# Spreading the second block's top 16, cutting the convolution into pieces, and a norm column that holds epsilon

## The chip, the cores and the metric

One core of a Trainium2 chip runs the whole kernel in one launch. The metric is the device time of that launch in microseconds (us). Five engines work side by side, each through its own queue in order: TensorE (PE in the profile; its weight loads are PEld), VectorE (DVE), ScalarE (ACT), GpSimd (POOL) and SyncE (SP), which issues most of the DMA transfers.

## The reference

Two blocks of two layers each work on x, 256 tokens of 1024 channels, in float32. What matters for the change:

```python
def _layer(x, ...):                      # the first block, layers l0 and l1
    h = _rms_norm(x, norm_g)             # x * rsqrt(mean(x*x) + 1e-6) * g
    proj = h @ w_in                      # a, a_glu, z_conv, c_q, ..., u_sg, v_sg, z_sg
    y_conv = _conv_branch(a, a_glu, ...) * silu(z_conv)   # 31 taps, causal, depthwise
    y_mla = _mla_branch(...) * silu(z_mla)
    y_sg = _sgu_branch(u_sg, v_sg, ...) * silu(z_sg)
    y = concat([rms_norm(y_conv), rms_norm(y_mla), rms_norm(y_sg)])
    return x + y @ w_out

def peer_ffn(h, w_q, sub_keys, u_tab, v_tab):   # the second block, twice
    scores = einsum(h @ w_q, sub_keys)
    s1, i1 = top_k(scores[..., 0, :], 16);  s2, i2 = top_k(scores[..., 1, :], 16)
    top_s, top_pos = top_k(s1[:, None] + s2[None, :], 16)   # per token and head, of 8 heads
    gate = softmax(top_s)                # 16384 experts, 128 chosen per token
    act = gelu(einsum(u_tab[idx], h))
    return einsum(gate * act, v_tab[idx])
```

The second block runs: norm, hgrn2 mixer, norm, peer; norm, rglru ("lru") mixer, norm, peer; and a last norm. The modulation vectors of its layers (`cond @ w_ada + b_ada`) do not depend on x.

## The kernel before, in words

The stages are l0, l1, hg, p0, lru, p1 and fin. x lies in one tile for the whole run, in two blocks b of 128 tokens. Weights come through a ring of four 1 MB slots (`wp`, tile w) and a ring of twelve 4 KB-per-partition buffers (`rp`, tile r). Outside the peer loops the order of each engine's queue is planned when the program is built: of the instructions that are ready, the one that stands first in the program goes first; `behind()` queues a group behind the last instructions that `mod_hT` or `split_T` marked.

**A norm of x** (`rms_x`, lines 301 to 307): ScalarE squares the block and sums it (line 305), GpSimd scales the sum and adds epsilon (line 166, in `pow`), then raises it to -0.5 (line 170); VectorE multiplies x by it (line 313). There are 14: two blocks in each of l0, l1, hg, p0, lru, p1 and fin; the two of fin end in line 1471.

**A layer of the first block** (`first_layer`, 457 to 576). A weight unit `W(u)` is split into a high and a low half (ScalarE line 226, VectorE line 227), for three matmuls per product (254 to 256). Behind the attention's inputs come the spatial gate's projections (`sgu`), the scores, then `conv` (729 to 743): 31 taps for two halves of the channels, 62 VectorE instructions in a chain (737, 740). Behind it in the program stand three gate units (9, 10, 11: two weight splits each), `values` with the softmax's transposes, unit 6, the branch norms and products (`branch`, 553 to 565), modulation rows (`ada`, line 267), and `conv_out` (745 to 777), which needs the convolution's result cv from line 755 on. `out_proj` ends the layer.

**The peer stage** (`peer`, 1174 to 1461) ends in two loops of 128 units written out in order under `manual_schedule`. In the u loop, unit j loads 128 rows of the u table (half of a 1 MB slot), TensorE multiplies it with the last 160 tokens (line 1335), ScalarE applies gelu (`u_act`). The first 96 tokens (`TS`) instead fetch their own 128 rows each through GpSimd's indirect DMA (`fetch`, line 1293, six ahead) and take them one row of 128 at a time on VectorE (`own`, line 1305), paced by unit. Each fetch takes a buffer of `rp`. Block 1's top 16 also runs within this loop: for each head, `keys` (VectorE's maxima and indices, then sums of candidates on GpSimd, lines 1104 to 1117) and `sums` (1123 to 1127); then `slot_rows` (1142 to 1159, two buffers of `rp`), `slot_weights` (exponential on ScalarE, line 1133; VectorE 1134 to 1136), and `slot_columns(1)` on TensorE (1166, 1170). `own_rows(r)` copies a group of tokens on ScalarE into a buffer of `rp` (1276, 1277) and turns it on TensorE (1281). From unit `G0` on, `hot`, `meet` and `put` set the expert weights of four tokens every second unit. The v loop follows (line 1434).

The lru stage's steps (line 1079) each begin with one modulation unit, two instructions of line 267, from the third step on.

Of the kernel before, what the change touches and what calls it, by code (L numbers as in the profile page):

```python
# [137 lines left out]
class Kernel:  # L138
# [35 lines left out]

    def setup(self):
        nc, A, k = self.nc, self.A, self.keep
        self.x = self.t(k, (P, 2, D), "x")
        self.mhalf = self.t(k, (P, 1), "mhalf")
        nc.vector.memset(self.mhalf, -0.5)

        nc.scalar.activation(self.t(k, (P, 1), "warm"), self.mhalf, AF.Square)
        for b in range(2):
            nc.sync.dma_start(self.x[:, b], A["x"][b * P:(b + 1) * P])
        self.cst = self.t(k, (P, NCONST - 1024), "cst")
        nc.scalar.dma_start(self.cst[:, :256], A["consts"][:, :256])
        self.cols = self.t(k, (P, NCOLS), "cols")
        nc.scalar.dma_start(self.cols, A["cols"])
        self.ident = self.cst[:, K_ID:K_ID + P]
        self.mask = self.cst[:, K_MASK:K_MASK + P]
        self.iota = self.cst[:, 256:256 + P]  # L190
        self.cos = self.cst[:, K_COS - 1024:K_COS - 1024 + 32].rearrange("p (b h) -> p b h", b=2)
        self.sin = self.cst[:, K_SIN - 1024:K_SIN - 1024 + 32].rearrange("p (b h) -> p b h", b=2)
        self.c31 = self.t(k, (P, 8), "c31", U32)
        nc.vector.memset(self.c31, 31)
        self.ones = self.t(k, (P, S), "ones")
        nc.vector.memset(self.ones, 1.0)
        self.mod = [self.t(k, (P, 48), f"mod{l}") for l in range(2)]
        self.ada_todo = [(l, j) for l in range(2) for j in range(0, 48, 2)]
        self.cond = None
# [98 lines left out]
        at = R1[(name, layer)] - R1[("conv_pw_b", layer)]  # L298
        return self.rows[:, at:at + n]

    def rms_x(self, b, out):

        nc = self.nc
        rs = self.t(self.keep, (P, 1), "rs", bufs=2)
        nc.scalar.activation(out, self.x[:, b], AF.Square, accum_out=rs)  # L305
        self.rstd(rs, rs, D)
        return rs

    def norm_x(self, b):

        xn = self.rp.tile([P, D], F32, name="r")
        rs = self.rms_x(b, xn)
        self.nc.vector.tensor_scalar(xn, self.x[:, b], rs, None, op0=ALU.mult)
        return xn

    def mod_hT(self, pool, l, h, hT=None, parts=True):
# [140 lines left out]
    def first_layer(self, l):  # L457
        nc, tc = self.nc, self.tc
        W = lambda u: self.w3(f"win{l}", u * SLOT)
        with tc.tile_pool(name=f"l{l}", bufs=1) as pl, tc.tile_pool(name=f"m{l}", bufs=2) as pm:  # L460
# [75 lines left out]
            with tc.tile_pool(name=f"b{l}", bufs=1) as pb:  # L536
                y = self.t(pb, (P, 2, D), "y")
                zc = self.t(pb, (P, 2, 256), "zc")
                z = self.t(pb, (P, 2, 768), "z")
                sgu = self.sgu(l, pb, pm, wm, wuv)  # L540
                sc, rl = self.scores(pb, pm, qT, kT, rq)
                cv = self.conv(l, pb, yp)
                def gate_unit(u, dst):

                    w = W(u)
                    for b in range(2):
                        nc.scalar.activation(dst[:, b], self.proj3(w, b), AF.Copy)

                for n in range(3):
                    gate_unit(9 + n, z[:, :, n * 256:(n + 1) * 256])  # L550
                yT = self.t(pb, (P, 8, S), "yT")

                def branch(c0, n):

                    for b in range(2):
                        ys = y[:, b, c0:c0 + n]
                        zs = z[:, b, c0 - 256:c0 - 256 + n] if c0 else zc[:, b]
                        nc.scalar.activation(zs, zs, AF.Silu)
                        nc.vector.tensor_tensor(ys, ys, zs, op=ALU.mult)
                        junk = self.t(pl, (P, D), "junk", BF16)  # L560
                        ss = self.t(pm, (P, 1), "bss")
                        nc.scalar.activation(junk[:, :n], ys, AF.Square, accum_out=ss)
                        self.rstd(ss, ss, n)
                        nc.vector.tensor_scalar(ys, ys, ss, None, op0=ALU.mult)
                        self.transpose_T(ys, yT, c0 // P, n // P, b, lambda c: self.col("branch_norm_g", c, l))

                self.values(pm, sc, rl, v, y)
                gate_unit(6, zc)
                branch(256, 512)
                sgu(y)  # L570
                self.ada(ADA[l][1])
                branch(768, 256)
                self.conv_out(l, pb, cv, wm, y)
                branch(0, 256)
                self.ada(len(self.ada_todo) - (34, 18)[l])
                self.out_proj(f"wout{l}", yT, (1, 2, 3, 0), 1)
# [150 lines left out]
                                            rl[:, hs, b:b + 1].to_broadcast([P, 2, 64]), op=ALU.mult)  # L727

    def conv(self, l, pl, yp):
        nc = self.nc  # L730
        cv = self.t(pl, (P, 2, S), "cv")
        o = [None, None]
        for j in range(31):
            for f in range(2):
                dst = cv[:, f] if j == 30 else self.t(pl, (P, S), f"cvb{f}", bufs=2)
                if j == 0:
# [3 lines left out]
                    nc.vector.scalar_tensor_tensor(dst, yp[:, f, j:j + S], self.col("conv_w", f * 31 + j, l), o[f],  # L740
                                                   op0=ALU.mult, op1=ALU.add)
                o[f] = dst
        return cv

    def conv_out(self, l, pl, cv, wm, y):

# [246 lines left out]
    def lru(self):  # L993
        nc, tc = self.nc, self.tc
        first = [self.w1("lruin", n * SLOT) for n in range(2)]
        with tc.tile_pool(name="lr", bufs=1) as pl, tc.tile_pool(name="lrm", bufs=2) as pm:
# [81 lines left out]
            heads = self.proj_blocks(first, mT)  # L1078
            for step in "x0 x1 x2 g0 x3 y0 y1 g1 d0 s0 y2 y3 d1 s1".split():
                k, n = step[0], int(step[1])  # L1080
                self.ada(1 if step not in ("x0", "x1") else 0)
                if k == "x":
                    x_unit(n)
                elif k == "y":
                    y_unit(n)
                elif k == "g":
                    gates(n, 0)
                    gates(n, 1)
                elif k == "d":
                    decay(n)  # L1090
                else:
                    for f in range(4):
                        scan(n, f)
# [80 lines left out]
    def peer(self, l):  # L1174
# [9 lines left out]
        with ExitStack() as ctx:  # L1184
# [132 lines left out]
            with tc.manual_schedule():  # L1317
# [56 lines left out]

                NG = TD // 4
                AHEAD = 6
                G0 = 34
                k = 0
                for j in range(P):
                    u_mm(j)  # L1380
                    if j in (2, 26):
                        b = j // 26
                        late = self.slot_rows(pn, tif[b], ts[b], tp[b])
                    if j:
                        u_act(j - 1)
                    if j in (6, 30):
                        self.slot_weights(pn, late[0])

                    for f, at in ((sums, (9, 12, 14, 16, 19, 21, 23, 25)), (keys, (7, 9, 12, 14, 17, 19, 21, 23))):
                        if j in at:  # L1390
                            f(at.index(j), 1)
                    if j == 9:
# [5 lines left out]
                            fetch(i)  # L1398
                    if j == 12:
                        own_rows(0)  # L1400
                    if j == 32:
                        self.slot_columns(1, *late, slots)
                        c1.close()
                        wts["b"] = self.t(pool("pw"), (P, P - JW, TD), "Wb")
                    if j in (40, 72):
                        own_rows(1 if j == 40 else 2)
                    if j >= 13 and k < TS and (j - 13) * TS >= k * 112:
                        own(k)
                        fetch(k + AHEAD)
# [53 lines left out]
    def final(self, out):  # L1463
# [3 lines left out]
        nc.scalar.dma_start(rows, bass.AP(tensor=r.tensor, offset=r.offset + R_FINAL, ap=[[0, P], [1, D]]))  # L1467
        for b in range(2):
            o = self.rp.tile([P, D], F32, name="r")
            rs = self.rms_x(b, o)  # L1470
            nc.vector.scalar_tensor_tensor(o, self.x[:, b], rs, rows, op0=ALU.mult, op1=ALU.mult)  # L1471
            nc.sync.dma_start(out[b * P:(b + 1) * P], o)

# [37 lines left out]
```

## Time and profile before

| | us |
|---|---|
| median of three runs | 2140.9 (2137.68 to 2143.72) |
| the profiled execution | 2138.78 |
| its span | 2137.1 |
| mean granted TensorE clock in it | 0.969 of full speed |

The profile is one execution. A view of waits names, for each engine, which instruction of another engine released it; a timeline lists instructions by start, merged where equal ones follow each other, with the idle time before them and what ended it in brackets; the table of stretches gives each engine's busy time between two times. L12 is line 12 of the kernel.

### The profile page before, as it was taken

How to read it: one execution, taken by the hardware profiler on the slowest of the kernel's cores; microseconds unless marked ns; L12 is line 12 of the kernel's file. 1: busy time of each engine (PE TensorE's matmuls, PEld its weight loads, DVE VectorE, ACT ScalarE, POOL GpSimd, SP SyncE). 2: the span in 40 equal slices, each digit the busy share in tenths (PEclk: the TensorE clock that was granted, in tenths of full speed). 3: DMA queues.
4: the chain of work that ended last, by engine and by line, in shares of the span. 5: the costliest groups of instructions: out<-in, count | busy, mean ns of one | idle time of the engine just before them, and what ended most of it. 6: DMA issues, size and time to landing. Idle time of an engine off the chain costs nothing. (4 is left out here: it accounts for less than half of the span.)

```text
span 2137.1 us, 35449 instructions
## 1 busy us (share of the span) xinstructions
PE 1997.6 (93%) x13860; PEld 1871.6 (88%) x13860; DVE 1402.8 (66%) x3072; ACT 630.4 (29%) x1697; POOL 636.1 (30%) x696
## 2 busy tenths in 40 slices
PE   6978978999999979999999997999979999999997
PEld 6664777788869979999999997969979999999997
DVE  7697687587648776788444446967786788544444
ACT  4442462354523224432000001754224433000000
POOL 0202111011001464444344440001373444244442
PEclk9989999999999989999999998999989999999999
DMA  9537617443413899999999999643799999999996
GB/s 347 219 149 283 240 64 308 148 140 95 149 50 139 339 339 367 343 369 389 368 414 415 415 415 387 247 154 119 263 357 371 354 360 378 370 416 415 415 415 267
DMA packets 123719, 630.01 MB, mean 295 GB/s; under 512 B 13728, under 2 KB 14368, under 8 KB 79264
## 3 DMA queue, kind: packets, MB, share of 16 engines
q1 hardware_dynamic: 66960, 422.87, 51.4%
q0 software_dynamic: 55296, 201.35, 24.4%
q10 hardware_dynamic: 1296, 3.53, 0.5%
q8 instruction: 109, 1.79, 0.3%
q14 instruction: 58, 0.48, 0.1%
HBM read 626.65 MB, written 1.05 MB: 294 GB/s over the span
## 5 line engine op out<-in xcount | busy, mean ns | idle before, releaser
L1335 PE MATMUL ps<-hT,w 128*128 128x160 f32 x4096 | 573.0, 299 | 0.3 <-issue 0.2
L1335 PEld LDWEIGHTS ps<-hT,w 128*128 128x128 f32 x4096 | 560.3, 190 | 0.8 <-issue 0.8
L1314 DVE SCALAR_TENSOR_TENSOR hl<-r,asl,hl 128x1024 f32<-128x1024 f32 x186 | 239.1, 1285 | 312.5 <-DMA r<-v,ids 302.9
L1434 PE MATMUL acc<-Wa,w 128*128 128x160 f32 x2560 | 348.4, 299 | 0.0
L1434 PEld LDWEIGHTS acc<-Wa,w 128*128 128x128 f32 x2560 | 347.9, 190 | 0.0
L1293 POOL DMA_INDIRECT r<-v,ids x192 | 240.2, 1251 | 339.7 <-PE acc L1434 263.6
L1293 POOL DMA_INDIRECT r<-urow,ids x192 | 257.7, 1342 | 260.4 <-DVE r L1305 138.0
L1305 DVE SCALAR_TENSOR_TENSOR r<-r,hh 128x1024 f32<-128x1024 f32 x192 | 232.5, 1219 | 1.4 <-DMA r<-urow,ids 1.4
L1434 PE MATMUL acc<-Wb,w 128*128 128x160 f32 x1536 | 209.6, 299 | 0.3 <-DMA w<-v 0.3
L1434 PEld LDWEIGHTS acc<-Wb,w 128*128 128x128 f32 x1536 | 208.8, 190 | 0.5 <-DMA w<-v 0.5
L1453 ACT ACTIVATE hT<-acc,mod 128x256 f32<-128x256 f32 x8 | 3.5, 474 | 573.5 <-DVE hT L1455 573.5
L1355 ACT ACTIVATE r<-r,hl 128x128 f32<-128x128 f32 x320 | 102.2, 390 | 224.2 <-DVE r L1352 224.2
L254 PE MATMUL ps<-hh,r 128*128 128x256 f32 (+1 forms) x464 | 135.4, 292 | 5.3 <-ACT r L226 4.2
L256 PE MATMUL ps<-hh,r 128*128 128x256 f32 (+1 forms) x464 | 132.8, 286 | 6.0 <-DVE r L227 6.0
L255 PE MATMUL ps<-hl,r 128*128 128x256 f32 (+1 forms) x464 | 132.9, 287 | 0.5 <-DVE hl L377 0.5
L227 DVE TENSOR_TENSOR r<-w,r 128x1024 fp32r<-128x1024 f32 (+1 forms) x82 | 96.9, 1201 | 32.3 <-ACT r L226 30.5
L267 DVE SCALAR_TENSOR_TENSOR w<-w,crow 128x1024 f32<-128x1024 f32 x96 | 114.0, 1219 | 2.9 <-ACT crow L819 2.1
L226 ACT ACTIVATE r<-w 128x1024 fp32r<-128x1024 f32 (+1 forms) x82 | 83.6, 1037 | 80.0 <-PE ps L255 33.9
L1352 DVE TENSOR_TENSOR r<-cst,hl 128x1024 f32<-128x1024 f32 x80 | 97.6, 1220 | 0.0
L254 PEld LDWEIGHTS ps<-hh,r 128*128 128x128 f32 (+1 forms) x464 | 88.8, 192 | 7.1 <-ACT r L226 5.0
L256 PEld LDWEIGHTS ps<-hh,r 128*128 128x128 f32 (+1 forms) x464 | 88.4, 191 | 7.2 <-DVE r L227 6.9
L255 PEld LDWEIGHTS ps<-hl,r 128*128 128x128 f32 (+1 forms) x464 | 88.7, 192 | 1.4 <-DVE hl L377 0.8
(382 smaller groups left out, 2930.2 us busy)
## 6 DMA issues: line engine op xcount, KB each, us to landing
w<-u SPq DMA_DIRECT2D x128, 1024.0 KB
w<-v SPq DMA_DIRECT2D x128, 1024.0 KB
w<-ada SPq DMA_DIRECT2D x48, 1024.0 KB
w<-win SPq DMA_DIRECT2D x24, 1024.0 KB
r<-hgin SPq DMA_DIRECT2D x40, 512.0 KB
w<-wq SPq DMA_DIRECT2D x12, 1024.0 KB
r<-wout SPq DMA_DIRECT2D x16, 512.0 KB
r<-wmid SPq DMA_DIRECT2D x12, 384.0 KB
```

The costliest lines, as they stand in the source:

```text
L227: self.nc.vector.tensor_tensor(lo, x, hi.bitcast(F32), op=ALU.subtract)
L254: mm(ps, a[0], b[0], start=start, stop=False)
L255: mm(ps, a[0], b[1], start=False, stop=False)
L256: mm(ps, a[1], b[0], start=False, stop=stop)
L267: nc.vector.scalar_tensor_tensor(x, x, 1.0, self.cond, op0=ALU.mult, op1=ALU.mult, accum_out=m[:, j + i:j + i + 1])
L1293: g = nc.gpsimd.indirect_dma_start(out=x, out_offset=None, in_=A[f"urow{l}"] if k < TS else vrow, in_offset=at)
L1305: nc.vector.scalar_tensor_tensor(x, x, 1.0, hrep[r % 2], op0=ALU.mult, op1=ALU.mult, accum_out=asl[:, g:g + 1])
L1314: nc.vector.scalar_tensor_tensor(accs[r % 2], x, asl[:, g:g + 1], accs[r % 2], op0=ALU.mult, op1=ALU.add)
L1335: nc.tensor.matmul(ps, u[:, c], hT[:, c, TS:], start=c == 0, stop=c == 7)
L1352: nc.vector.tensor_tensor(o, self.iota[:, None, None].to_broadcast([P, 2, 4, P]), slots[:, 1:3, k:k + 4, None].to_broadcast([P, 2, 4, P]), ...
L1355: nc.scalar.activation(o[:, 1, t], o[:, 1, t], AF.Copy, scale=slots[:, 0, k + t:k + t + 1])
L1434: mm = nc.tensor.matmul(acc[c // 2][:, c % 2, TS:], v[:, c * P:(c + 1) * P], W(j), start=j == 0 and c % 2 == 0, stop=False, skip_group_che ...
```

## The change

x gets eight more columns; the first of them holds the root of 1024 times epsilon, so that the Square's sum over 1025 columns already has epsilon in it, and the constant factor goes into the multiplication that follows (or, in fin, into a small instruction of VectorE). `conv` returns a function that issues a given number of its 31 steps; `first_layer` calls it behind each of three gate units (6 each), behind unit 6 (7) and behind the first branch (6). In the lru stage the modulation units are queued behind `mod_hT`'s last instructions. In the u loop block 1's `sums` and `keys` are spread to unit 28 in place of 25, `slot_rows` moves from unit 26 to 29, `slot_weights` from 30 to 34, `slot_columns` from 32 to 39, `own_rows(1)` from 40 to 37, and `G0` from 34 to 40.

```diff
--- before.py
+++ after.py
@@ -174,11 +174,14 @@
 
     def setup(self):
         nc, A, k = self.nc, self.A, self.keep
-        self.x = self.t(k, (P, 2, D), "x")
+
+        self.xe = self.t(k, (P, 2, D + 8), "x")
+        self.x = self.xe[:, :, :D]
         self.mhalf = self.t(k, (P, 1), "mhalf")
         nc.vector.memset(self.mhalf, -0.5)
 
         nc.scalar.activation(self.t(k, (P, 1), "warm"), self.mhalf, AF.Square)
+        nc.gpsimd.memset(self.xe[:, :, D:D + 1], (D * EPS) ** 0.5)
         for b in range(2):
             nc.sync.dma_start(self.x[:, b], A["x"][b * P:(b + 1) * P])
         self.cst = self.t(k, (P, NCONST - 1024), "cst")
@@ -298,19 +301,20 @@
         at = R1[(name, layer)] - R1[("conv_pw_b", layer)]
         return self.rows[:, at:at + n]
 
-    def rms_x(self, b, out):
+    def rms_x(self, b):
 
         nc = self.nc
         rs = self.t(self.keep, (P, 1), "rs", bufs=2)
-        nc.scalar.activation(out, self.x[:, b], AF.Square, accum_out=rs)
-        self.rstd(rs, rs, D)
+        sq = self.rp.tile([P, SLOT], BF16, name="r")[:, :D + 1]
+        nc.scalar.activation(sq, self.xe[:, b, :D + 1], AF.Square, accum_out=rs)
+        nc.gpsimd.tensor_tensor(rs, rs, self.mhalf, op=ALU.pow)
         return rs
 
     def norm_x(self, b):
 
         xn = self.rp.tile([P, D], F32, name="r")
-        rs = self.rms_x(b, xn)
-        self.nc.vector.tensor_scalar(xn, self.x[:, b], rs, None, op0=ALU.mult)
+        rs = self.rms_x(b)
+        self.nc.vector.tensor_scalar(xn, self.x[:, b], rs, float(D) ** 0.5, op0=ALU.mult, op1=ALU.mult)
         return xn
 
     def mod_hT(self, pool, l, h, hT=None, parts=True):
@@ -539,7 +543,8 @@
                 z = self.t(pb, (P, 2, 768), "z")
                 sgu = self.sgu(l, pb, pm, wm, wuv)
                 sc, rl = self.scores(pb, pm, qT, kT, rq)
-                cv = self.conv(l, pb, yp)
+                cv, conv = self.conv(l, pb, yp)
+
                 def gate_unit(u, dst):
 
                     w = W(u)
@@ -548,6 +553,7 @@
 
                 for n in range(3):
                     gate_unit(9 + n, z[:, :, n * 256:(n + 1) * 256])
+                    conv(6)
                 yT = self.t(pb, (P, 8, S), "yT")
 
                 def branch(c0, n):
@@ -566,7 +572,9 @@
 
                 self.values(pm, sc, rl, v, y)
                 gate_unit(6, zc)
+                conv(7)
                 branch(256, 512)
+                conv(6)
                 sgu(y)
                 self.ada(ADA[l][1])
                 branch(768, 256)
@@ -727,10 +735,17 @@
                                             rl[:, hs, b:b + 1].to_broadcast([P, 2, 64]), op=ALU.mult)
 
     def conv(self, l, pl, yp):
+
         nc = self.nc
         cv = self.t(pl, (P, 2, S), "cv")
-        o = [None, None]
-        for j in range(31):
+        o, left = [None, None], list(range(31))
+
+        def steps(n):
+            for j in left[:n]:
+                step(j)
+            del left[:n]
+
+        def step(j):
             for f in range(2):
                 dst = cv[:, f] if j == 30 else self.t(pl, (P, S), f"cvb{f}", bufs=2)
                 if j == 0:
@@ -740,7 +755,8 @@
                     nc.vector.scalar_tensor_tensor(dst, yp[:, f, j:j + S], self.col("conv_w", f * 31 + j, l), o[f],
                                                    op0=ALU.mult, op1=ALU.add)
                 o[f] = dst
-        return cv
+
+        return cv, steps
 
     def conv_out(self, l, pl, cv, wm, y):
 
@@ -1078,7 +1094,9 @@
             heads = self.proj_blocks(first, mT)
             for step in "x0 x1 x2 g0 x3 y0 y1 g1 d0 s0 y2 y3 d1 s1".split():
                 k, n = step[0], int(step[1])
-                self.ada(1 if step not in ("x0", "x1") else 0)
+                if step not in ("x0", "x1"):
+                    with self.behind():
+                        self.ada(1)
                 if k == "x":
                     x_unit(n)
                 elif k == "y":
@@ -1374,19 +1392,19 @@
 
                 NG = TD // 4
                 AHEAD = 6
-                G0 = 34
+                G0 = 40
                 k = 0
                 for j in range(P):
                     u_mm(j)
-                    if j in (2, 26):
-                        b = j // 26
+                    if j in (2, 29):
+                        b = j // 29
                         late = self.slot_rows(pn, tif[b], ts[b], tp[b])
                     if j:
                         u_act(j - 1)
-                    if j in (6, 30):
+                    if j in (6, 34):
                         self.slot_weights(pn, late[0])
 
-                    for f, at in ((sums, (9, 12, 14, 16, 19, 21, 23, 25)), (keys, (7, 9, 12, 14, 17, 19, 21, 23))):
+                    for f, at in ((sums, (10, 13, 15, 18, 20, 23, 25, 28)), (keys, (7, 10, 13, 15, 18, 20, 23, 25))):
                         if j in at:
                             f(at.index(j), 1)
                     if j == 9:
@@ -1398,12 +1416,12 @@
                             fetch(i)
                     if j == 12:
                         own_rows(0)
-                    if j == 32:
+                    if j == 39:
                         self.slot_columns(1, *late, slots)
                         c1.close()
                         wts["b"] = self.t(pool("pw"), (P, P - JW, TD), "Wb")
-                    if j in (40, 72):
-                        own_rows(1 if j == 40 else 2)
+                    if j in (37, 72):
+                        own_rows(1 if j == 37 else 2)
                     if j >= 13 and k < TS and (j - 13) * TS >= k * 112:
                         own(k)
                         fetch(k + AHEAD)
@@ -1467,7 +1485,8 @@
         nc.scalar.dma_start(rows, bass.AP(tensor=r.tensor, offset=r.offset + R_FINAL, ap=[[0, P], [1, D]]))
         for b in range(2):
             o = self.rp.tile([P, D], F32, name="r")
-            rs = self.rms_x(b, o)
+            rs = self.rms_x(b)
+            nc.vector.tensor_scalar(rs, rs, float(D) ** 0.5, None, op0=ALU.mult)
             nc.vector.scalar_tensor_tensor(o, self.x[:, b], rs, rows, op0=ALU.mult, op1=ALU.mult)
             nc.sync.dma_start(out[b * P:(b + 1) * P], o)
 

```

## Rows read from the trace of the kernel before

**Rows 1.** What TensorE waited for: for whom, us in all, times, longest.

```profile
PE ps L255 <- DVE r L227: 30.2, 2, 15.1
PE ps L1166 <- DVE wk L1136: 29.0, 2, 15.3
```

**Rows 2.** Timeline of VectorE, layer 0: start us, us, engine, line, operation, count.

```profile
129.17 6.73 DVE L740 SCALAR_TENSOR_TENSOR cvb<-yp,cols,cvb 128x256 f32<-128x256 f32 x17
...
136.61 6.90 DVE L227 TENSOR_TENSOR r<-w,r 128x1024 fp32r<-128x1024 f32 x6
...
176.41 0.75 DVE L755 SCALAR_TENSOR_TENSOR cv<-ps,cv 128x256 f32<-128x256 f32 x2
```

**Rows 3.** Stretches: us, busy per engine, granted clock, DMA share, GB/s.

```profile
core 0: us, PE busy (x) PEld busy (x) DVE busy (x) ACT busy (x) POOL busy (x), PEclk, DMA share, GB/s
122.84:203.00 80.16, 61.37 (x328) 44.62 (x329) 66.19 (x150) 28.29 (x68) 10.17 (x15) 0.87 0.65 252
137.89:142.00 4.11, 4.11 (x19) 4.11 (x20) 4.11 (x4) 0.00 (x0) 0.00 (x0) 0.51 0.47 146
309.40:385.80 76.40, 58.59 (x324) 43.59 (x324) 59.32 (x140) 26.60 (x67) 8.26 (x14) 0.89 0.68 257
771.20:776.80 5.60, 5.59 (x40) 5.54 (x41) 5.60 (x11) 0.68 (x2) 4.68 (x4) 0.50 0.88 290
1100.00:1150.00 50.00, 50.00 (x373) 50.00 (x372) 21.31 (x17) 0.00 (x0) 23.11 (x18) 1.00 1.02 414
1339.00:1400.00 61.00, 61.00 (x362) 56.04 (x361) 60.88 (x111) 44.64 (x63) 0.39 (x4) 1.00 0.65 243
```

**Rows 4.** Timeline of TensorE, first peer stage, around its gap.

```profile
739.71 16.19 PE L1335 MATMUL ps<-hT,w 128*128 128x160 f32 x118
771.21 0.45 PE L1166 MATMUL ps<-cst,wk 128*128 128x128 f32 x1 [15.31 <-DVE wk L1136]
```

**Rows 5.** Timeline of VectorE, first peer stage, before that gap ends.

```profile
756.90 0.24 DVE L1123 MAX8 ts<-cand 128x8 f32<-128x80 f32 x1 [0.78 <-POOL cand L1115]
...
769.08 1.22 DVE L1305 SCALAR_TENSOR_TENSOR r<-r,hh 128x1024 f32<-128x1024 f32 x1
...
770.23 0.28 DVE L1134 TENSOR_REDUCE wsm<-wk 128x8 f32<-128x128 f32 x1
```

**Rows 6.** Timeline of GpSimd, same stage: one fetch.

```profile
768.28 1.68 POOL L1293 DMA_INDIRECT r<-urow,ids  x1 [1.28 <-DVE r L1305]
```

**Rows 7.** Timeline of ScalarE, same stage: the copies of `own_rows(1)`.

```profile
793.32 0.84 ACT L1276 ACTIVATE r<-hT 128x768 f32<-128x768 f32 x1
794.05 0.41 ACT L1277 ACTIVATE r<-hT 128x256 f32<-128x256 f32 x1
```

**Rows 8.** The norms: timelines, groups by line, one line's durations (ns min/median/max).

```profile
2127.95 0.19 POOL L166 TENSOR_SCALAR rs<-rs 128x1 f32<-128x1 f32 x1 [26.99 <-ACT r L305]
2128.23 0.57 POOL L170 TENSOR_TENSOR rs<-rs,mhalf 128x1 f32<-128x1 f32 x1
2128.99 1.18 POOL L166 TENSOR_SCALAR rs<-rs 128x1 f32<-128x1 f32 x1 [0.19 <-ACT r L305]
...
2128.84 1.28 DVE L1471 SCALAR_TENSOR_TENSOR r<-x,rs,w 128x1024 f32<-128x1024 f32 x1 [1.56 <-POOL rs L170]
...
L166 POOL TENSOR_SCALAR rs<-rs 128x1 f32<-128x1 f32 x14 | 6.3, 451 | 180.3 <-ACT r L305 180.2
...
L313 DVE TENSOR_SCALAR r<-x,rs 128x1024 f32<-128x1024 f32 x12 | 9.0, 753 | 14.0 <-POOL rs L170 14.0
...
L894 DVE TENSOR_SCALAR hbE<-hf x4: 685/1112/1541, 415.5 to 520.1; 128x1024 f32<-128x1024 f32 x4
```

**Rows 9.** Timeline of VectorE, lru stage: first and last of ten, then line 227.

```profile
1309.81 1.22 DVE L267 SCALAR_TENSOR_TENSOR w<-w,crow 128x1024 f32<-128x1024 f32 x1
...
1332.97 1.22 DVE L267 SCALAR_TENSOR_TENSOR w<-w,crow 128x1024 f32<-128x1024 f32 x1
...
1339.02 1.23 DVE L227 TENSOR_TENSOR r<-w,r 128x1024 fp32r<-128x1024 f32 x1 [4.82 <-ACT r L226]
```

## The prediction

> **What bounds the kernel now.** I read the waits of TensorE over the whole span first, because a gap of the engine that carries the kernel shows a stage with another limit. Two causes make most of its idle time [rows 1]: in the two first layers it waits 15.1 us each for the low half of a split weight (line 227), and in the two peer stages 15.3 and 13.7 us for the slot weights of the second block (line 1136). No other wait comes near these four. The table by stretches tells what stands beside each gap. In layer 0 the gap lies from 122.84 to 137.89 us; VectorE is busy in it throughout, with convolution steps, 17 of them in one row before the six splits that TensorE wants [rows 2]. So the stage is bound there by the order of VectorE's queue, not by its total: from 122.84 to 203.0 it works 66.2 of 80.2 us, in the same part of layer 1 59.3 of 76.4 us [rows 3]. After each gap TensorE's granted clock is at the lower level for a while: 0.51 of full speed in the 4.1 us behind the first, 0.50 in 5.6 us behind the gap of the first peer stage [rows 3]; half of such a stretch is lost as well. In the peer's u loop TensorE is the bound apart from its gap. In its v loop the DMA engines are (busy share 1.02, 414 GB/s) [rows 3], and nothing in this change shortens that loop; a microsecond saved ahead of it moves it forward whole.
>
> **The convolution in pieces.** The 62 steps stay as they are; 17 take 6.73 us, so one costs 0.396 us [rows 2] and all of them 24.5 us per layer. They lose their place ahead of the weight splits of gate units 10, 11 and 6: now six steps (12 instructions, 4.8 us) are asked for behind each unit. A ready instruction that stands earlier in the program goes first, so the splits overtake the steps. What can vanish per layer is the gap and the slow clock behind it: 15.05 + 4.1 / 2 = 17.1 us in layer 0 and about 17.7 us in layer 1. But VectorE's work is not less. It has 80.2 - 66.2 = 14.0 us of idle time in that part of layer 0 and 76.4 - 59.3 = 17.1 us in layer 1 [rows 3]; that is the most that either layer can shrink, unless modulation work (line 267) slides into the next stage. Some of that idle time belongs to the serial tail of the convolution branch, from line 755 at 176.4 us on [rows 2], and stays. I take 11 us for layer 0 and 13 us for layer 1, nearer to the upper end, because the tail's holes can be filled by the modulation work that is displaced. Bounds: 3 us for both together, if VectorE's queue is what ends the layer anyway, and 31 us. Next late is VectorE itself.
>
> **The spread top 16.** Block 1's chain on VectorE is: eight rounds of keys and sums, `slot_rows`, `slot_weights`, and between them one row of `own` per u unit. TensorE used to meet `slot_columns(1)` behind unit 32, at 755.9 us, and stood until 771.2 us [rows 4]. A unit takes 2.2 us (118 matmuls, 16 to a unit, in 16.19 us [rows 4]). The change moves `slot_columns(1)` behind unit 39, seven units later, but also puts four more `own` rows ahead of `slot_weights(1)` (18 in place of 14, by the pacing rule), 1.15 us each [rows 5], and lets the first round come behind `own_slots`, which costs about 1 us and saves about as much in later waits such as the 0.78 us before a sum [rows 5]. Line 1134 then starts at 770.2 + 4.6 = 774.8 us. ScalarE's exponential, now at unit 34, waits for the first step of `slot_rows` and holds up the gelus behind it, as before; TensorE has four PSUM banks in hand for that. The step that catches TensorE is now another one: `own_rows(1)` moved from unit 40 to 37. Its ScalarE copy needs a buffer of the ring of 12, which the trace shows being handed on in order: the fetch issued at 768.28 us waited for the `own` that freed its buffer [rows 6]. Counting the ring through the program, `own_rows(1)` inherits the buffer of `own(16)`, the next but one ahead of `slot_weights(1)`, done at about 774.8 - 1.15 = 773.7 us. TensorE gets there after unit 37, at 755.9 + 5 x 2.2 = 766.9 us. Add 1.15 us for the two copies (0.84 and 0.41, overlapping [rows 7]) and it goes on at about 774.9 us: a stall of 8.0 us in place of 15.3, with the same slow clock behind it. Behind it are two more units, by whose end line 1136 is done, so `slot_columns(1)` costs no second wait. Gain 7.3 us per peer stage, 14.6 in all. Bounds per stage: 4 us, if three more sums wait 0.78 us and the slip ahead of them is not won back, and 18.1 us (15.3 + 2.8), if the buffer comes early. The hot columns start six units later and end at unit 122 of 128; VectorE is not behind there, so I cost that at nothing; if it were, the v loop would start late by the last product.
>
> **The norms.** Of the 14 norms of x each loses the GpSimd step of line 166 (6.3 us in all) and keeps that of line 170 [rows 8]. Twelve stand ahead of line 313, where VectorE waits 14.0 us for them [rows 8]; there 0.28 us comes off, from the start of the one step at 2127.95 us to that of the other at 2128.23 us, 3.4 us in all; in the last two, line 1471, a small VectorE step is added that gives it back. The two-operation form of line 313 is not in the trace on x; the nearest row, line 894, has two operations on 128x1024 and a minimum of 0.685 us against 0.753 us for line 313 [rows 8], so I cost it at nothing. The Square reads one column more and writes to a ring buffer of its own, released at once. I take 3 us, between -1 and 6.3.
>
> **Modulation behind the mark in the lru stage.** Ten of these instructions, 1.22 us each, ran from 1309.81 us on between the steps of the norm [rows 9], some of them in front of a step that was ready: that gives back up to 4 us. They move into VectorE's queue behind the last split; 4.82 us of idle time there [rows 9] hold four, and six (6.9 us) go into a stretch with 60.9 of 61.0 us busy [rows 3]. TensorE is the bound there and has a few microseconds in hand. I take +1.5, between -4 and +4.
>
> **Sum.** 11 + 13 + 14.6 + 3 + 1.5 = 43 us. The profiled execution took 2138.8 us (span 2137.1), 2.1 us under the median of the runs, 2140.9; from that median the forecast is 2097.
>
> **A rule against the change.** The trace shows a GpSimd step of line 166 that took 0.19 us at 2127.95 us and 1.18 us at 2128.99 us, where VectorE ran line 1471 beside it, two SBUF tensors in, from 2128.84 us for 1.28 us; both ended within 0.05 us [rows 8]. By the same hold a convolution step that now runs beside the branch norms could hold each of their eight GpSimd steps per layer for up to its 0.40 us: 3.2 us per layer, 6.4 in all, and 2103. The Trainium skill states this in "SBUF — State Buffer", section "Who interferes with whom": a VectorE instruction with two SBUF inputs keeps out a GpSimd instruction that reads SBUF until it ends. Here the trace agrees, with 1.18 against 0.19 us.
>
> **Rivals.** (a) Both gaps close whole: 14 + 17 for the layers, 18.1 and 15.3 for the peers, 4.5 for the rest, 69 us: 2072. For it: VectorE's idle time would just do; against it: `own(16)`. (b) The layers gain little, since ready convolution steps are drawn forward again, or VectorE ends the layers: 3 + 14.6 + 3 = 21 us: 2120. For it: VectorE is solid from 122.84 on. (c) Slower: the last 26 convolution instructions (10.3 us) fall behind 18 modulation instructions (20.7 us) and two splits (2.4 us), serial ahead of `conv_out`. TensorE comes to that point 17 us earlier than at 176.4, about 159.3 us; with 33.4 us it is 192.7, 16 us late in each layer, +32 - 18 = +14: 2155. It decides from the point where the last step ends over 9 us later than line 755 began before. Against it: steps are always ready and fill holes. (d) The GpSimd steps held: 2103.
>
> **How the numbers follow.** Chances: forecast 0.52, (d) 0.10, (a) 0.15, (b) 0.15, (c) 0.08. The range 2072 to 2122 leaves out (c), and half each of what lies beyond (a) and (b). A measurement tells 0.3% (6.4 us) from no change: faster 0.91, same 0.03, slower 0.06.
>
> **What would show it.** Right: the waits for line 227 of 15.1 us gone, with convolution rows between the splits; the wait for line 1136 replaced by one of about 8 us for line 1276 or 1277; ten fewer microseconds of each first layer; `rs` with one GpSimd row. Wrong: a wait for line 227 left in the layers, a wait for `cv` at `conv_out`, no TensorE gap in the u loop at all, or lruout's matmuls waiting for `hs`.

## The result, and the profile after

The changed kernel took 2106.1 us (median of five runs, 2102.6 to 2109.1) against 2141.2: a ratio of 0.983, interval 0.982 to 0.985. Timed again beside the last experiments it took 2102.5, ratio 0.981 (0.980 to 0.983). So it won 35 to 40 us, where 43 was forecast, and both times lie in the range. The profiled executions have spans of 2100.9 and 2101.1 us, against 2137.1.

The stages, worked out from the traces: each from the first norm of x in it (line 313 before, 317 after) to the next one, layer 0 from the start of the span, the peer stages cut at the first and last matmul of their loops.

| us | l0 | l1 | hg | p0 head | p0 u loop | p0 v loop | end of p0 to lru | lru | p1 head | p1 u loop | p1 v loop | fin |
|---|---|---|---|---|---|---|---|---|---|---|---|---|
| before | 205.7 | 184.6 | 226.5 | 63.7 | 342.9 | 282.3 | 16.3 | 114.0 | 63.5 | 340.9 | 281.8 | 14.8 |
| after | 197.8 | 175.3 | 226.0 | 62.7 | 334.6 | 282.2 | 11.4 | 115.4 | 64.0 | 335.4 | 281.8 | 14.4 |
| after, second profile | 201.1 | 175.5 | 226.0 | 62.7 | 334.5 | 282.2 | 8.4 | 115.3 | 64.0 | 335.4 | 281.8 | 14.4 |

The waits of TensorE in the changed kernel, the view of [rows 1] (for whom, us in all, times, longest); the lines have moved: 1299 was 1281, 393 was 389, 1446 was 1428.

```profile
PE ps L1299 <- ACT r L1295: 20.1, 4, 8.7
PE ps L393 <- DVE y L570: 11.2, 7, 4.1
PE acc L1446 <- DVE hl L1332: 3.3, 1, 3.3
```

Both rows of [rows 1] are gone: no wait for line 227 (now 230) at the gate units, and none for the slot weights. Four short waits for that line in the first 60 us of layer 0 are still there (line 259, 6.6 us, 2.8 at the longest; 6.0 before, line 256). In place of the two rows stand the wait at `own_rows` that the forecast named (8.3 and 8.7 us; the other two of its four, 1.5 us each at unit 72, were there before), and two that it did not name: for line 570, the scaling of a branch by its norm, at the end of the first layers, and 1.9 us in each of these layers for the softmax's transposes (line 726).

The first peer stage, answering to [rows 4 to 7]: timelines of TensorE, ScalarE and VectorE (start, duration, engine, line, operation, idle time before it and what ended that).

```profile
756.29 1.97 PE L1299 MATMUL ps<-cst,r 128*128 128x128 f32 x8 [8.30 <-ACT r L1295]
...
755.09 0.84 ACT L1294 ACTIVATE r<-hT 128x768 f32<-128x768 f32 x1 [8.93 <-DVE r L1323]
755.84 0.40 ACT L1295 ACTIVATE r<-hT 128x256 f32<-128x256 f32 x1
...
753.76 1.29 DVE L1323 SCALAR_TENSOR_TENSOR r<-r,hh 128x1024 f32<-128x1024 f32 x1
754.98 1.21 DVE L1323 SCALAR_TENSOR_TENSOR r<-r,hh 128x1024 f32<-128x1024 f32 x1
756.13 0.27 DVE L1152 TENSOR_REDUCE wsm<-wk 128x8 f32<-128x128 f32 x1
```

The copy of `own_rows(1)` starts when the next to last `own` ahead of the slot weights ends (753.76 + 1.29 = 755.05): that of `own(16)`. The u loop begins 18.7 us earlier than before (661.8 against 680.5), so on the timeline of the kernel before TensorE reached this point at 756.29 - 8.30 + 18.7 = 766.7 us and left it at 775.0; the forecast said 766.9 and 774.9.

The end of layer 0, answering to [rows 2]: VectorE's timeline,

```profile
150.38 0.88 DVE L755 SCALAR_TENSOR_TENSOR cv<-yp,cols,cvb 128x256 f32<-128x256 f32 x2
156.12 1.21 DVE L270 SCALAR_TENSOR_TENSOR w<-w,crow 128x1024 f32<-128x1024 f32 x1
...
164.30 1.22 DVE L270 SCALAR_TENSOR_TENSOR w<-w,crow 128x1024 f32<-128x1024 f32 x1
...
165.45 0.76 DVE L565 TENSOR_TENSOR y<-y,z 128x256 f32<-128x256 f32 x2
166.18 0.17 DVE L765 MEMSET om<- 128x128 f32 x1
...
174.23 0.76 DVE L771 SCALAR_TENSOR_TENSOR cv<-ps,cv 128x256 f32<-128x256 f32 x2 [0.42 <-PE ps L768]
```

and TensorE's:

```profile
152.80 13.90 PE L256 MATMUL acc<-r,yT 128*128 128x512 f32 x32
...
172.81 1.38 PE L768 MATMUL ps<-cv,om 128*128 128x256 f32 x4
```

The convolution is done at 151.3 us, but its next step, line 771 (755 before), starts at 174.2: ahead of it stand eight modulation instructions in a row (156.12 to 165.45), then the last product of the gate branch and the constant that `conv_out` needs. TensorE works off what it has of the output projection meanwhile (line 256), and then waits for the branches; its product with that constant (line 768), which line 771 needs, comes behind these in its queue. Its waits by that end of the layer, before (140 to 203 us) and after (140 to 195), then both in layer 1 (317 to 388 and 317 to 373):

```profile
PE ps L389 <- DVE y L564: 1.6, 2, 1.4
...
PE ps L393 <- DVE y L570: 6.4, 3, 4.1
...
PE ps L389 <- DVE y L564: 1.3, 2, 0.7
...
PE ps L393 <- DVE y L570: 4.7, 4, 2.4
```

The table of stretches, as in [rows 3]: the same part of each layer, then the stretches behind two of the new gaps.

```profile
core 0: us, PE busy (x) PEld busy (x) DVE busy (x) ACT busy (x) POOL busy (x), PEclk, DMA share, GB/s
122.84:195.00 72.16, 62.47 (x329) 44.05 (x328) 62.95 (x150) 25.85 (x68) 9.33 (x15) 0.93 0.70 255
302.90:369.70 66.80, 58.71 (x326) 42.41 (x325) 58.62 (x144) 23.72 (x64) 9.22 (x14) 0.97 0.75 271
169.40:173.40 4.00, 3.97 (x8) 1.99 (x9) 3.12 (x7) 0.34 (x1) 0.62 (x1) 0.59 0.88 320
188.80:194.00 5.20, 5.20 (x8) 2.45 (x9) 3.74 (x8) 0.37 (x1) 0.00 (x0) 0.50 1.00 370
```

VectorE is still idle 72.16 - 62.95 = 9.2 us of that part of layer 0 (14.0 before) and 66.80 - 58.62 = 8.2 us of that of layer 1 (17.1 before). Behind the gaps that end at 168.5 and 187.6 us the granted clock is 0.59 and 0.50: the lower level for most of the one stretch and all of the other, and at that level half of TensorE's speed is lost.

### The profile page after: what moved, and what is told of

The parts are those of the page before. It is cut to its first block, busy times and chain, and to the rows that moved or that the text cites. A ratio compares the mean times of both kernels' runs of the same rounds, so it can differ in the third digit from the quotient of the medians.

```text
span 2100.9 us, 35398 instructions
## 1 busy us (share of the span) xinstructions
PE 1998.1 (95%) x13860; PEld 1871.6 (89%) x13860; DVE 1403.3 (67%) x3068; ACT 617.7 (29%) x1684; POOL 626.3 (30%) x683
## 5 line engine op out<-in xcount | busy, mean ns | idle before, releaser
L1311 POOL DMA_INDIRECT r<-v,ids x192 | 232.0, 1208 | 346.4 <-PE acc L1452 255.1
L1311 POOL DMA_INDIRECT r<-urow,ids x192 | 252.7, 1316 | 243.3 <-DVE r L1323 133.6
```

The lines of the kernel that those rows point to most:

```text
L1311: g = nc.gpsimd.indirect_dma_start(out=x, out_offset=None, in_=A[f"urow{l}"] if k < TS else vrow, in_offset=at)
```

## The experiments

A median below stands beside the ratio to the kernel before, timed on the same chip; "saved" is what that ratio lacks to 1, times 2141. The changed kernel is "after".

**Each part alone.** Four kernels, each the kernel before with one part of the change, as it stands in the diff: the convolution in pieces (all hunks on `conv`), the spread top 16 (all hunks of the u loop), the norm column (`setup`, `rms_x`, `norm_x`, fin) and the lru stage's modulation. One hunk of each:

```diff
-                cv = self.conv(l, pb, yp)
+                cv, conv = self.conv(l, pb, yp)
...
-                G0 = 34
+                G0 = 40
...
-        nc.scalar.activation(out, self.x[:, b], AF.Square, accum_out=rs)
-        self.rstd(rs, rs, D)
+        sq = self.rp.tile([P, SLOT], BF16, name="r")[:, :D + 1]
+        nc.scalar.activation(sq, self.xe[:, b, :D + 1], AF.Square, accum_out=rs)
+        nc.gpsimd.tensor_tensor(rs, rs, self.mhalf, op=ALU.pow)
...
-                self.ada(1 if step not in ("x0", "x1") else 0)
+                if step not in ("x0", "x1"):
+                    with self.behind():
+                        self.ada(1)
```

> The kernel before with the convolution in pieces alone. If the changed kernel's parts add up, as its stages suggest (layer 0 shorter by 7.5 us, layer 1 by 9.2 us, about 1 us of it from the norms), this gives 15 to 16 us: about 2125.5. If the parts help each other (a layer that is bound elsewhere once the norms are slow), it gives under 12 us. As first forecast (11 + 13), it would give 24 us: 2117.

> The kernel before with the spread top 16 alone (sums, keys, slot rows, slot weights, slot columns, own_rows(1), G0). Adding up: 8.5 us in the first peer stage and 5.6 in the second, 14.1 us: about 2127. TensorE's gap in the u loop 8.3 to 8.7 us, at own_rows(1). If the earlier end of the layers or the modulation moves were part of the gain, clearly less.

> The kernel before with the norm column alone. My sum: 12 norms by 0.28 us, 3 us: 2138. Lower bound: no change, if a held GpSimd step had been hidden (the second norm of each pair runs while TensorE still works on the first); upper 5 us.

> The kernel before with the modulation of the lru stage queued behind the splits, alone. From the stages of the changed kernel: 5.0 us won between the end of the v loop and the first norm of the lru stage's input, less about 0.5 that the norm column gives there, and 1.4 us lost in the stage's body: 3 us net, 2138. The first forecast was 1.5 us.

| | median us | ratio (95% interval) | saved us |
|---|---|---|---|
| convolution in pieces | 2126.2 | 0.9941 (0.9920 to 0.9962) | 12.6 |
| spread top 16 | 2125.1 | 0.9931 (0.9915 to 0.9948) | 14.8 |
| norm column | 2133.1 | 0.9969 (0.9959 to 0.9980) | 6.6 |
| lru modulation | 2137.7 | 0.9982 (0.9968 to 0.9996) | 3.9 |

Together 37.9 us, the size of the whole change (35 to 40): the parts add up within their intervals, and the shortfall lies in the convolution, 12.6 us (8.1 to 17.1 by its interval) where 24 were forecast. In its profile layer 0 is 5.8 us shorter and layer 1 7.1, and TensorE waits for the branch's scaling as in the changed kernel (4.1 us at the longest), so neither the other parts nor their meeting causes that wait. In the profile of the spread alone the two u loops are 8.1 and 6.1 us shorter, with this gap:

```profile
771.63 1.75 PE L1281 MATMUL ps<-cst,r 128*128 128x128 f32 x7 [8.31 <-ACT r L1277]
```

**Is it the ring buffer?** `own_rows(1)` behind unit 46 or behind unit 22, in the changed kernel.

```diff
-                    if j in (37, 72):
-                        own_rows(1 if j == 37 else 2)
+                    if j in (46, 72):
+                        own_rows(1 if j == 46 else 2)
```

and, for unit 22,

```diff
-                    if j in (37, 72):
-                        own_rows(1 if j == 37 else 2)
+                    if j in (22, 72):
+                        own_rows(1 if j == 22 else 2)
```

> The changed kernel with own_rows(1) behind unit 46 in place of 37. Theory: its ScalarE copy waited for the ring buffer of own(16). Moved, TensorE goes on at 747.99 us through two more units and meets slot_columns(1) at about 752.3 us, whose weights VectorE ends at 756.96: a gap of about 4.6 us for the slot weights in place of 8.3 at the own_rows transposes; about 4 us per peer stage, 8 in all: 2098. Rival (VectorE's lag, not the ring, holds this point): a gap of 8 us stays, under one name or another, and the time stays at 2106.

> The changed kernel with own_rows(1) behind unit 22. If the wait at own_rows(1) is for a ring buffer that comes in turn (behind unit 22 it is one of a row that was done long before), TensorE doesn't stop there, and the gap is again about 4.6 us at slot_columns(1): about 2098, as with unit 46. If the copy waits for something else that ends at about 755 us (the ScalarE queue, hT), TensorE stops at unit 22 or the gap at unit 37 stays as it is.

They took 2099.9 us, 0.9809 (0.9794 to 0.9824), and 2097.8, 0.9797 (0.9777 to 0.9817). TensorE's timeline, first peer stage, unit 46 and then unit 22:

```profile
761.94 0.30 PE L1184 MATMUL ps<-cst,wk 128*128 128x128 f32 x1 [3.77 <-DVE wk L1154]
...
759.39 0.30 PE L1184 MATMUL ps<-cst,wk 128*128 128x128 f32 x1 [3.33 <-DVE wk L1154]
```

In both the gap of 8.3 us is gone, and the next late thing is the slot weights, 3.8 and 3.3 us (expected 4.6); with unit 22 the first product of a hot column (line 1380) waits as well in the second peer stage, 3.1 us. Moved nine units later or fifteen earlier, the copy does not wait; that leaves the buffer that comes round at unit 37. The u loops are 331.6 and 330.8 us with unit 46, 330.8 and 333.0 with unit 22, against 334.6 and 335.4. By the runs' times neither kernel is apart from the second timing of the changed one (0.980 to 0.983). Some of the gain comes back behind the v loop: with unit 46 TensorE waits 4.6 us there for the last row's sum (line 1332), where after waited 3.3 and 1.8.

**Everything later.** As with unit 46, and the slot columns and hot columns later as well.

```diff
-                G0 = 40
+                G0 = 43
...
-                    if j == 39:
+                    if j == 42:
...
-                    if j in (37, 72):
-                        own_rows(1 if j == 37 else 2)
+                    if j in (46, 72):
+                        own_rows(1 if j == 46 else 2)
```

> As the last, and slot_columns(1) behind unit 42, the hot columns from 43. TensorE gets to unit 42 at about 758.9 us, after the weights (756.96): no gap over 1 us in either u loop, and no half clock behind it. Gain over the changed kernel 8.3 + 8.7 + 4 us of clock = 20 us at most, 16 to 20: about 2088. Rival: the hot columns end at unit 125 of 128, and the v loop waits for the last product; then up to 5 us of it per stage come back.

2109.0 us, 0.9849 (0.9830 to 0.9869): the u loops are 340.4 and 338.0 us, worse than after. The slot weights cost TensorE nothing any more, but the first product of a hot column does. TensorE's row, two of VectorE's ahead of it, and the stretch (columns as before):

```profile
781.23 2.08 PE L1380 MATMUL acc<-r 128*128 128x128 f32 x8 [10.09 <-ACT r L1373]
...
768.95 1.23 DVE L1323 SCALAR_TENSOR_TENSOR r<-r,hh 128x1024 f32<-128x1024 f32 x1 [2.53 <-DMA r<-urow,ids]
...
779.52 1.22 DVE L1370 TENSOR_TENSOR r<-cst,hl 128x1024 f32<-128x1024 f32 x1
...
760.00:780.00 20.00, 11.13 (x101) 10.88 (x99) 9.41 (x17) 0.99 (x3) 10.35 (x8) 0.83 1.02 415
```

The hot column of unit 43 (line 1370) stands in VectorE's queue behind the `own` rows up to that unit, and these wait for their fetches, 1.6 to 2.5 us each, with the DMA engines full. My rival here, an end of the hot columns too near the end of the loop, was not it. The order of the queue alone could also have made the gap, so the last test on this takes DMA traffic away. It is the kernel with everything later, and the second u unit of each pair uses the first one's rows; the other half of the table is left out.

```diff
-                pairs[name] = self.slot(A[f"{name}{l}"][:, j * D:(j + 2) * D])
+                pairs[name] = self.slot(A[f"{name}{l}"][:, j * D:(j + (1 if name == "u" else 2)) * D])
-            return pairs[name][:, j % 2 * D:(j % 2 + 1) * D]
+            return pairs[name][:, :D] if name == "u" else pairs[name][:, j % 2 * D:(j % 2 + 1) * D]
```

> The changed kernel with own_rows(1) at 46, slot_columns at 42 and the hot columns from 43, and the u table loaded at half: the second unit of each pair uses the first one's rows (the other half of the table is left out). The slow one of the earlier runs had a wait of 10.1 us at the first hot product, behind VectorE's rows, which waited 1.6 to 2.5 us each for their fetch, with the DMA share at 1.02. If the u stream and the row fetches together are what makes those rows late, halving the u stream takes the DMA share under 0.9, the rows' waits and the 10.1 us gap under 2 us: the u loops come to about 326 us each, 2090 or less. If the order of VectorE's queue alone makes the gap, it stays at 8 to 10 us.

2100.5 us, 0.9789 (0.9764 to 0.9814). VectorE's waits for rows from 755 to 782 us, in the kernel with everything later and in this one, and TensorE's row here:

```profile
DVE r L1323 <- DMA r<-urow,ids: 8.2, 4, 2.5
...
DVE r L1323 <- DMA r<-urow,ids: 0.3, 1, 0.3
...
773.72 1.37 PE L1380 MATMUL acc<-r 128*128 128x128 f32 x8 [0.42 <-ACT r L1373]
```

10.09 us became 0.42, in a kernel with the same order of instructions: the u stream is what made the rows late. The rest of what I expected missed. The DMA share from 760 to 773.5 us was 1.03 all the same, since the fetches take what is left to them. By queue (packets, MB, share of 16 engines; q1 loads the u table, q0 fetches rows) that stretch reads, in the kernel with everything later, in this one, and in the one with unit 46 alone:

```profile
q1 hardware_dynamic: 486, 3.59, 64.0%
q0 software_dynamic: 550, 2.00, 36.9%
...
q0 software_dynamic: 983, 3.56, 65.8%
q1 hardware_dynamic: 532, 1.96, 36.1%
...
q0 software_dynamic: 965, 3.51, 64.8%
q1 hardware_dynamic: 288, 2.10, 37.3%
```

The engines are full in all three; the rows' part of them differs. In the last, as I read it, TensorE's stop of 3.8 us for the slot weights holds the table back. And the u loops of the test came to 332.5 and 331.4 us rather than 326, since `own_rows` stops TensorE again, for 2.0 us at unit 46 and 3.8 at unit 72.

**What ends a first layer?** The modulation that stands ahead of the gate branch is put behind the last one; and, in another kernel, modulation in these layers is made thin.

```diff
-                self.ada(ADA[l][1])
                 branch(768, 256)
                 self.conv_out(l, pb, cv, wm, y)
                 branch(0, 256)
+                self.ada(ADA[l][1])
```

and, where the first layers ask for modulation, with `cut` = 64 of 1024 columns (the rest of that sum is left out),

```diff
-                x = w[:, i * D:(i + 1) * D]
+                x = w[:, i * D:i * D + cut]
```

> The changed kernel with the modulation rows that stand in front of the gate branch in the first layers (5 and 4 units, ten and eight instructions) put behind the last branch. Theory: in the changed kernel the end of a first layer is a chain of small steps (branch norm, conv_out, branch norm) that starts 14 us late since VectorE works off modulation first; TensorE's gaps in that chain (7.7 us in layer 0, 6.1 in layer 1) and the half clock behind them (5.1 and 1.9 us) shrink by half or more: gain 6 to 14 us, about 2097. Rival, the one of the forecast: VectorE's total ends the layer; then its work is only moved, and the time stays within 3 us of 2106.

> The changed kernel with the modulation instructions of the two first layers reading 64 of 1024 columns (the rest of that sum is left out): their 1.15 us each fall to about 0.15 us, in the same places. It asks whether VectorE's total ends those layers in the changed kernel. If it does, or if TensorE's gaps at the end of a layer come from modulation queued in front of the chain there, those gaps (1.8 and 4.1 us in layer 0, 1.1 and 2.4 us in layer 1) go below 1 us: 8 us off layer 0 and 5 off layer 1, 2093. If the chain is long by its own steps (GpSimd's, ScalarE's and the transposes), the gaps stay and the layers gain under 3 us each: 2102 to 2106.

The first took 2098.4 us, 0.9796 (0.9777 to 0.9815), which is below the first timing of the changed kernel and not apart from its second; the second 2077.8, 0.9691 (0.9674 to 0.9709). TensorE's waits for the branch's scaling in layer 0 (140 to 194.5 us), with modulation moved and with it thin, and its wait at the next norm (194 to 212 us) with modulation moved:

```profile
PE ps L393 <- DVE y L570: 2.5, 3, 1.1
...
PE ps L393 <- DVE y L570: 2.0, 2, 1.6
...
PE ps L377 <- DVE r L317: 6.3, 2, 3.2
```

So the modulation in front of the chain is what makes the new wait: moved, 6.4 us fall to 2.5 in layer 0, and 4.7 to 2.1 in layer 1. The wait at line 782, in the same chain, rises meanwhile from 0.8 to 2.3 and from 1.4 to 2.1 us. And in layer 0 the move is no gain: the moved instructions now stand in front of the next norm, where TensorE waits 6.3 us in place of 3.5, and the stage is 197.6 us long (197.8 and 201.1 before the move). Layer 1 gains 2.8 us. Thin, the sixty instructions take 220 in place of 1217 ns:

```profile
L270 DVE SCALAR_TENSOR_TENSOR w<-w,crow 128x64 f32<-128x64 f32 x60 | 10.4, 220 | 13.3 <-DMA w<-ada 9.0 <-ACT crow L835 4.3
```

VectorE has some 60 us less to do, and the two layers are 182.4 and 166.8 us long, 24 us shorter than in the changed kernel's first profile. Some 10 of the 24 are won in their first halves: TensorE comes to the transposes of line 671 5.2 us earlier in layer 0 and 4.4 in layer 1. My expectation of 13 us asked only for the gaps at the end. That VectorE's total is part of what bounds these layers fits this, but it is not shown: a thin instruction is also a shorter hold for whatever stands behind it in the queue. Reordering gives about 3 us by the stages' lengths, less work gives 24.

**The best together**, `own_rows(1)` behind unit 22 and the moved modulation, with the changed kernel timed again beside it.

> Both moves that gained, together: own_rows(1) behind unit 22, and the modulation of the first layers behind the last branch. They lie in different stages: the gains over the changed kernel (8.3 and 7.7 us by the medians, 5.8 and 4.2 by the profiled spans) add to 10 to 16 us: 2090 to 2096. If the gain of the modulation move was only scatter of the clock in the layers, 2098.

> The changed kernel itself again, beside the others: 2106, ratio to the kernel before 0.983. A second profile of it shows which of its layer gaps and half-clock stretches are the same each time (the gaps) and which move (the stretches, by my reading of the runs so far: 3 us per layer either way).

2089.0 us, 0.9752 (0.9739 to 0.9766), against 2102.5 for the changed kernel on the same chip: 13 us faster than it, with intervals well apart, and 53 faster than the kernel before. Its u loops are 330.7 and 330.9 us, its layers 197.8 and 173.8. The moved modulation adds 9 us by time to the kernel with unit 22 alone, and 4 us to its two layers (371.6 against 375.3); where the rest comes from is open.

## Why the prediction was right, and where it was off

**The sum.** 35 to 40 us came of 43. That it came so near is in part luck: the largest term was twice too large, and the norms and the lru stage measured 6 us more than forecast. (The last subtraction is off by one as well: 2140.9 - 43 is 2098.) One of the signs, ten fewer microseconds of each first layer, did not come: 7.9 and 9.3 in the table.

**Spread top 16: right in mechanism and size.** 14.6 us forecast; 14.8 alone by time; in the table the two u loops are together 13.8 and 13.9 us shorter. The stalls were 8.3 and 8.7 us for 8.0, at the line that was named; the first ended with the `own` that was named. The lower clock stayed behind them as said (0.50 in the 3.7 us from 756.3). No second wait for the slot columns came, as worked out. The halves were not the 7.3 us each of the forecast but 8.3 and 5.5: it took the old gap of the first stage, 15.3 us, for both, and that of the second was 13.7.

**Convolution in pieces: the direction right, the term too large.** 24 us forecast, 12.6 alone. The step that failed is the choice within the bounds, "because the tail's holes can be filled by the modulation work that is displaced". The two waits of [rows 1] for line 227 went whole, 30.2 us; but of the 14.0 us of idle time in that part of layer 0 only 14.0 - 9.2 = 4.8 filled (the 8.0 us by which it shrank are these and 66.2 - 63.0 = 3.2 us of VectorE's work that now lies outside it), and of the 17.1 us in layer 1 17.1 - 8.2 = 8.9. The modulation did not fall into the tail's holes; by the rule that the step standing earlier in the program goes first, which I had used for the splits, it went ahead of the tail, and TensorE waited there 4.8 us more in layer 0 and 3.4 more in layer 1, with the lower clock behind it, and 1.9 us in each for the softmax's transposes. That the modulation put the tail's waits there is shown by moving it (line 726 waits its 1.9 us even so); that it makes up the whole shortfall is not, since the move won only some 3 us of layer time. In [rows 2] nothing of it shows; as I read it, the old gap gave the tail its lead. Rival (b), VectorE's total, may hold the rest: the thin kernel fits it, and does not tell it from the order. Rival (c), the conv tail late, was in the wrong place: cv was done at 151.3 us, and line 771 started at 174.2, not later than line 755 before (176.4).

**Norms.** 3 us forecast. VectorE's wait for the GpSimd step, [rows 8], fell from 14.0 to 11.1 us, and line 317 with two operations costs what line 313 did:

```profile
L317 DVE TENSOR_SCALAR r<-x,rs 128x1024 f32<-128x1024 f32 x12 | 9.0, 753 | 11.5 <-POOL rs L310 11.1
```

2.9 of the 3.4 us, and nothing for the second operation: right. Alone the part saved 6.6 us by time (4.3 to 8.8 by its interval) and 3.9 by the spans of one pair of profiles; what makes the rest is open.

**Lru modulation.** +1.5 forecast, 3.9 measured alone (0.9 to 6.9, which holds the forecast). The stretch ahead of the stage's norm was 3.0 us shorter in that kernel, as the row [rows 9] with its "up to 4" let expect. Whether the cost that I took off for VectorE's full queue came can't be read: the stage's body is 112.9 us there and 114.0 before, but 113.0 to 115.6 in nine profiles whose code for this stage is one and the same. The spans of that pair of profiles are equal, 2137.1 us, since layer 0, with unchanged code, took 3.0 us longer.

**The rule against the change** (d) did not bite. Beside convolution steps the branch norm's GpSimd steps took 0.21 and 0.67 us, against 0.19 and 0.57 in [rows 8]:

```profile
147.06 0.87 DVE L755 SCALAR_TENSOR_TENSOR cvb<-yp,cols,cvb 128x256 f32<-128x256 f32 x2
147.38 0.21 POOL L166 TENSOR_SCALAR bss<-bss 128x1 f32<-128x1 f32 x1 [31.03 <-ACT junk L568]
147.67 0.67 POOL L170 TENSOR_TENSOR bss<-bss,mhalf 128x1 f32<-128x1 f32 x1
```

Only these two of the eight steps of a layer met a convolution step, and the hold cost 0.1 us of the 0.4 that I had priced for each. The hold itself is still there in fin, where a step beside line 1490 (1.28 us) took 1.45 us and the one ahead of it 0.57. The Trainium skill's rule ("SBUF — State Buffer", section "Who interferes with whom") agrees with that row; the price I gave it for the convolution was too high.

## What to carry to other kernels

An idle total of an engine is a limit, not a gain: before taking it, see what the queue's rule puts into the idle time, and whether that stands ahead of a chain another engine will need. In a loop written out in order, look for the buffer that a moved step inherits; here a step that waited for its turn in a ring lost that wait when it was moved, in either direction. And when a stall goes, ask which stream it had held back: with none left ahead of the hot columns, the u table took 64% of the DMA engines and the row fetches ran late.

## What the runs showed of the hardware

The same gap does not always cost the same clock. In layer 0 TensorE waits 1.9 us for the softmax's transposes in both profiles of the changed kernel; the 4 us behind it, in the first and the second profile:

```profile
137.70:141.70 4.00, 4.00 (x36) 4.00 (x36) 4.00 (x13) 0.86 (x2) 0.00 (x0) 1.00 0.99 408
...
139.20:143.20 4.00, 3.99 (x21) 3.99 (x22) 2.88 (x7) 0.49 (x1) 0.00 (x0) 0.57 1.00 412
```

Every wait longer than 0.6 us in the later part of that layer is equal in the two profiles within 0.1 us, though in the second one of 0.55 us (line 718) stands just ahead of this gap. The granted clock over the whole layer is 0.96 and 0.94, and layer 0 took 197.8 and 201.1 us. A few microseconds of a layer's length are such scatter, so its gaps say more than its time. And the two streams of a u loop, table and rows, fill the DMA engines for much of it: in the changed kernel the share is 1.02 at 413 GB/s from 700 to 740 us, with TensorE busy throughout. A loop that looked bound by TensorE was close to a second bound.
